# Forming the lower half of a weight slab with an accumulating DMA instead of a VectorE subtraction

## The chip, the cores and the metric

The kernel runs on one core of one Trainium2 chip. The metric is the device time of one execution in microseconds (us); lower is better. The engines are TensorE (PE: matmuls, and PEld: its weight loads), VectorE (DVE), ScalarE (ACT), GpSimd (POOL) and SyncE (SP). Weights come from HBM by DMA; most loads are issued on SP's queue, a few on POOL's.

## The reference

A token sequence of 512 positions with 1024 channels goes through two blocks. The first block, to which the change is confined, runs four mixers on the same normalised input and adds them up, each under its own gate. Cut to what matters:

```python
h = rms_norm(x, g) * (1 + scale) + shift        # scale and shift from c @ ada_w
p = h @ w_in                                    # 1024 -> all branches and their gates
y0 = rwkv7(p[A]) @ rwkv_out                     # branch A, a recurrent mixer
y1 = spatial_gating(p[B]) @ sg_out              # branch B: gelu, layer norm, 128x128 mixing
y2 = short_conv(p[C]) @ conv_out                # branch C: three taps
y3 = s5(p[D]) @ glu                             # branch D: a state space scan, then a GLU
acc = sum(sigmoid(p[gate b]) * y_b for b in range(4))
x = x + modulation * (acc @ w_o)                # then a feed forward, then the second block
```

All of it is float32, and the result is wanted close to float32 accuracy.

## The kernel before, in words

Every float32 product is made of three products of shorter numbers. An operand is split into an upper half `hi`, rounded to the type that PE multiplies at full speed, and a lower half `lo`, which is what the rounding left over. `mm3` (L169) adds hi·hi, hi·lo and lo·hi in PSUM; the lo·lo term is left out.

Weights come in slabs of 128 partitions by 1024 numbers (512 KB). `wload` (L140) loads one: SP starts the DMA into `raw` (four buffers), ACT copies it into `whi`, rounded (L152), and DVE writes `wlo` = `raw` - `whi` (L153). `whi` and `wlo` have three buffers each. The activations are split in the same way by `split` (`hi` and `lo`).

`_merge` (L813) handles the gate and the output of one branch: for each of eight tiles m it loads a `w_in` slab, makes 24 matmuls into `gp`, lets ACT take their tanh into `th` (L836), makes 6 matmuls with the branch's out slab into `yp` (12 for branch 3) and adds the product to `acc[m]` on DVE. An out slab (`conv_out`, `sg_out`, the GLU weights, `rwkv_out`) serves four tiles; a fresh one is loaded ahead of m = 0 and m = 4 and keeps one of the three buffers for that long. Ahead of each tile one or two `_ada` steps are made: a slab of `ada_w`, which uses the same four `raw` buffers, and a dot product with it on DVE (L328).

`_first_block` (L1165) runs `_start` (two slabs and the split of x), the seven projections of branch A, the tables of branch D begun, branch C, branch B, merge 2, the shift of branch A (fourteen dots), the tables of branch D, branch D itself, then the recurrence of branch A with merges 1 and 3 as fill between its steps, merge 0, and `w_o`. In branch B, `svp` are its projections, `sgz` a chain on DVE that normalises them, and `sgm` the mixing matmuls that read it (L928). In branch D, `s5k` are matmuls whose result is sent through HBM by POOL's queue (`s5_scr`, then eight and four small transfers `s5_ti`) and copied by DVE into a table `s5_toe`; `s5y` (L1138) are the matmuls that read the table.

A scheduler (Tile) fixes the order of the instructions of each engine from the program; each engine then works through its own list in order, and a transfer is started by the engine in whose list it stands. The order in which the calls are written, the dependences and the number of buffers decide what may run ahead.

Of the kernel before, what the change touches and what calls it, by code (L numbers as in the profile page):

```python
# [25 lines left out]
KD = 8  # L26
# [66 lines left out]
class _Core:  # L93


    WMAX = 1040

    def __init__(self, ctx, tc, dram):
        self.tc, self.nc, self.dram = tc, tc.nc, dram
        pool = lambda **kw: ctx.enter_context(tc.tile_pool(**kw))  # L100
        self.const = pool(name="const", bufs=1)
        self.small = pool(name="small", bufs=3)
        self.wpool = pool(name="w", bufs=1)
        self.tag, self.npool = {}, 0
        self.scratch = pool(name="scr", bufs=1, space=DRAM)
        self.tap = lambda name, ap: None
# [35 lines left out]
    def wload(self, src, kt, cols, tag=None):  # L142

        nc, n = self.nc, kt * cols
        raw = self.wpool.tile([128, self.WMAX], F32, name="raw", tag="raw", bufs=4)
        if tag is None:
            hi = self.wpool.tile([128, self.WMAX], F32R, name="whi", tag="whi", bufs=3)
            lo = self.wpool.tile([128, self.WMAX], F32R, name="wlo", tag="wlo", bufs=3)
        else:
            hi, lo = self.g("whi", tag, F32R), self.g("wlo", tag, F32R)  # L150
        nc.sync.dma_start(raw[:, :n], src)
        nc.scalar.activation(hi[:, :n], raw[:, :n], AF.Copy)  # L152
        nc.vector.tensor_tensor(lo[:, :n], raw[:, :n], hi[:, :n].bitcast(F32), OP.subtract)  # L153
        v = lambda t: t[:, :n].rearrange("p (k c) -> p k c", k=kt)
        return v(hi), v(lo)

# [11 lines left out]

    def mm3(self, out, w, x, first=True, last=True):  # L169

        n, total = 0, 3 * len(w)
        for (wh, wl), (xh, xl) in zip(w, x):
            for a, b in ((wh, xh), (wh, xl), (wl, xh)):
                self.nc.tensor.matmul(out, lhsT=a, rhs=b, start=first and n == 0, stop=last and n == total - 1)  # L174
                n += 1

    def proj(self, src, x, kt=8, name="mm", w=None):

# [635 lines left out]
def _merge(K, b, outs, acc, ada, halves=None):  # L814

    nc, d = K.nc, K.dram
    name = ("rwkv_out", "sg_out", "conv_out", "s5_glu_w")[b]
    first = b == 2  # L820
    w = {}
    for m in range(8):
        if m % 4 == 0:
            w[0] = K.wload(d[name][m // 4], 2, 512)
            if b == 3:
                w[1] = K.wload(d[name][2 + m // 4], 2, 512)
        cs = slice((m % 4) * 128, (m % 4 + 1) * 128)
        for _ in range(1 if first else 2):
            next(ada, None)
        wh, wl = K.wload(d["w_in"][19 + 8 * b + m], 8, 128)  # L830
        gp = K.mm("gp")
        for k in range(KD):
            K.mm3(gp, [(wh[:, k], wl[:, k])], K.h[k:k + 1], first=k == 0, last=k == KD - 1)
            yield
        th = K.g("th", "tm")
        nc.scalar.activation(th, gp, AF.Tanh, scale=0.5)  # L836
        yp = K.mm("yp")
        K.mm3(yp, [(w[0][0][:, k, cs], w[0][1][:, k, cs]) for k in range(2)], outs)
        if b == 3:
            y2 = K.mm("yp2")  # L840
            K.mm3(y2, [(w[1][0][:, k, cs], w[1][1][:, k, cs]) for k in range(2)], outs)
            sg = K.g("sg", "tm")
            nc.scalar.activation(sg, y2, AF.Tanh, scale=0.5)
            nc.vector.scalar_tensor_tensor(sg, sg, 1.0, yp, OP.add, OP.mult)
            nc.vector.scalar_tensor_tensor(th, th, 1.0, sg, OP.add, OP.mult)
            nc.vector.scalar_tensor_tensor(acc[m], th, 0.5, acc[m], OP.mult, OP.add)
        elif first:
            nc.vector.scalar_tensor_tensor(acc[m], th, 1.0, yp, OP.add, OP.mult)
        else:
            nc.vector.scalar_tensor_tensor(th, th, 1.0, yp, OP.add, OP.mult)  # L850
            nc.vector.tensor_tensor(acc[m], acc[m], th, OP.add)
        if halves is not None:
            halves.append(K.split(acc[m], "mg", 0.5))
        yield
# [310 lines left out]
def _first_block(K):  # L1165
    nc, d = K.nc, K.dram
    with ExitStack() as mix:
# [5 lines left out]
        with K.tags(e=9, e4=8):  # L1173
            with K.tc.tile_pool(name="s5", bufs=1) as sp:
                x, g1, rs = _start(K)
                tiles = _rwkv(K, x, g1, rs)
                last = K.last
                with K.tc.issue_after(K.split_1):
                    z = _s5_setup(K, sp)
                yc = _conv_branch(K)  # L1180
                yb = _sg_branch(K, last)
                acc = [K.g(f"acc{m}", "xr") for m in range(8)]
                for _ in _merge(K, 2, yc, acc, ada):
                    pass
                la, pairs = _rwkv_shift(K, tiles, rs)
                with K.tc.issue_after(last):
                    tab = _s5_tables(K, sp, z)
# [13 lines left out]
        tags(mg=16)  # L1201
        for _ in _merge(K, 0, ya, acc, ada, mg):
            pass
        for m in range(8):
            K.tap(f"acc{m}", acc[m])
        K.xr = _load(K, "x", 8, "xr")
# [464 lines left out]
```

## Time and profile before

| | us |
|---|---|
| median of 3 runs | 2149.45 (2147.0 to 2153.06) |
| the profiled execution | 2149.2 |
| its span in the profile | 2147.4 |
| PE busy | 2094.6 |
| DVE busy | 1416.1 |
| ACT busy | 934.1 |
| POOL busy | 23.5 |

The span is the time from the first to the last instruction of the profiled execution; what lies around it is 1.8 us. Busy times are sums over the span of each engine. The names on either side of an arrow in a row are tiles: `gp<-hi,wlo` is a matmul that reads `hi` and `wlo` and writes `gp`. "2.05 <-DVE wlo L153" in brackets is idle time of the engine ahead of the instruction, and what ended it. PEclk is the share of TensorE's full clock that was granted.

### The profile page before, as it was taken

Reading aid. Unit: us, or ns where it says so; the run is one execution under the profiler, and the core shown is the slowest. Engines: PE = TensorE matmul, PEld = TensorE weight load, DVE = VectorE, ACT = ScalarE, POOL = GpSimd, SP = SyncE. Lnnn points to the kernel's source line nnn. Section 1 sums busy time; section 2 is a strip of 40 time slices with the busy share of each in tenths; the row PEclk is TensorE's granted clock in tenths of the full one; section 3 lists DMA queues with packets and bytes.
Section 4 is the critical chain, followed back from the end, with each engine's and each line's share of the span. In section 5 each row is a group of like instructions: output and inputs, shape, how many; then the busy total and the mean of one; then the engine's idle time right before and its main releaser. Section 6 shows DMA issues by size and latency. Waiting matters only on the chain.

```text
span 2147.4 us, 29518 instructions
## 1 busy us (share of the span) xinstructions
PE 2094.6 (98%) x11502; PEld 1692.7 (79%) x11502; DVE 1416.1 (66%) x2655; ACT 934.1 (43%) x1549; POOL 23.5 (1%) x44
## 2 busy tenths in 40 slices
PE   6999999999999999999999999999999999999998
PEld 4877787888888888897778888888887778788887
DVE  7997884755734344558876756747568867575775
ACT  3334432333523232446764423324469944243433
POOL 0010000000000000000000000000000000000000
PEclk9999999999999999999999999999999999999999
DMA  8355441123322232232212222232321122323222
GB/s 329 106 182 180 159 148 50 60 84 133 108 98 89 98 98 89 99 119 89 80 50 98 98 93 94 89 98 81 128 79 40 60 79 86 101 83 105 97 81 67
DMA packets 68091, 220.47 MB, mean 103 GB/s; under 512 B 8068, under 2 KB 11060, under 8 KB 67952
## 3 DMA queue, kind: packets, MB, share of 16 engines
q1 hardware_dynamic: 64704, 210.19, 29.6%
q0 software_dynamic: 2096, 6.30, 1.0%
q8 instruction: 91, 1.49, 0.3%
q10 hardware_dynamic: 1152, 2.10, 0.3%
q14 instruction: 48, 0.39, 0.1%
HBM read 215.25 MB, written 3.30 MB: 102 GB/s over the span
## 4 chain that ended last, share of the span: by engine, by line
PE 85%; DVE 6%; ACT 4%; DMA 2%; issue 1%; DVEq 0%; ACTq 0%; SPq 0%
PE mm L174 62%; PE gp L174 7%; PE vt L174 3%; PE yp L174 2%; DMA raw<-ada_w 2%; PE pT L1336 1%; DVE wlo L153 1%; PE po L1349 1%; PE fin L174 1%; PE s L1316 1%; PE s L1317 1%; ACT whi L152 1%; DVE raw L328 1%; ACT p L1324 1%; PE pmt L643 1%
## 5 line engine op out<-in xcount | busy, mean ns | idle before, releaser
L174 PE MATMUL mm<-hi,whi 128*128 128x512 f32 x2088 | 829.7, 398 | 19.1 <-ACT hi L161 17.8
L174 PE MATMUL mm<-hi,wlo 128*128 128x512 f32 x2088 | 830.5, 398 | 1.1 <-DVE wlo L153 1.1
L174 PE MATMUL mm<-lo,whi 128*128 128x512 f32 x2088 | 829.2, 397 | 1.1 <-DVE lo L165 0.5
L152 ACT ACTIVATE whi<-raw 128x1024 fp32r<-128x1024 f32 (+3 forms) x341 | 350.3, 1030 | 754.9 <-PE mm L174 600.9
L153 DVE TENSOR_TENSOR wlo<-raw,whi 128x1024 fp32r<-128x1024 f32 (+3 forms) x341 | 403.5, 1186 | 180.2 <-ACT whi L152 170.7
L174 PEld LDWEIGHTS mm<-hi,whi 128*128 128x128 f32 x2088 | 395.7, 190 | 110.3 <-ACT hi L161 20.8
L174 PEld LDWEIGHTS mm<-lo,whi 128*128 128x128 f32 x2088 | 394.9, 189 | 91.1 <-DVE lo L165 2.7
L174 PEld LDWEIGHTS mm<-hi,wlo 128*128 128x128 f32 x2088 | 394.7, 189 | 89.9 <-DVE wlo L153 2.0
L1521 DVE TENSOR_TENSOR u<-mm,spr 128x512 f32<-128x512 f32 x88 | 60.6, 688 | 82.5 <-PE mm L174 82.2
L174 PE MATMUL gp<-hi,wlo 128*128 128x512 f32 x256 | 102.7, 401 | 3.3 <-DVE wlo L153 3.3
L174 PE MATMUL gp<-hi,whi 128*128 128x512 f32 x256 | 104.1, 407 | 0.9 <-ACT whi L152 0.9
L174 PE MATMUL gp<-lo,whi 128*128 128x512 f32 x256 | 102.9, 402 | 0.0
L1541 DVE TENSOR_TENSOR x<-x,mm 128x512 f32<-128x512 f32 x48 | 33.0, 687 | 96.1 <-PE mm L174 96.1
L1240 DVE SCALAR_TENSOR_TENSOR x<-mm,modv,x 128x512 f32<-128x512 f32 x32 | 24.0, 751 | 91.0 <-PE mm L174 91.0
L1522 ACT ACTIVATE cv<-u,vecs 128x512 f32<-128x512 f32 x88 | 71.3, 810 | 3.4 <-DVE u L1521 3.2
L1524 DVE SCALAR_TENSOR_TENSOR cv<-u,vecs,cv 128x510 f32<-128x510 f32 x88 | 66.0, 750 | 3.1
L1523 DVE SCALAR_TENSOR_TENSOR cv<-u,vecs,cv 128x511 f32<-128x511 f32 x88 | 65.6, 746 | 2.3 <-ACT cv L1522 2.1
L1532 ACT ACTIVATE cth<-cv 128x512 f32<-128x512 f32 x44 | 27.8, 632 | 86.2 <-DVE cv L1524 86.2
L174 PEld LDWEIGHTS gp<-hi,wlo 128*128 128x128 f32 x256 | 48.4, 189 | 15.6 <-DVE wlo L153 5.1
L1324 ACT ACTIVATE p<-p,at_m 128x128 f32<-128x128 f32 (+1 forms) x96 | 53.4, 557 | 14.7 <-DVE at_m L1323 13.7
L174 PEld LDWEIGHTS gp<-hi,whi 128*128 128x128 f32 x256 | 48.6, 190 | 13.4 <-ACT whi L152 1.8
L174 PEld LDWEIGHTS gp<-lo,whi 128*128 128x128 f32 x256 | 48.6, 190 | 10.6 <-issue 0.4
(532 smaller groups left out, 2612.1 us busy)
## 6 DMA issues: line engine op xcount, KB each, us to landing
raw<-w_up SPq DMA_DIRECT2D x88, 512.0 KB, 3.3
raw<-ffn_w SPq DMA_DIRECT2D x64, 512.0 KB, 3.3
raw<-w_in SPq DMA_DIRECT2D x49, 512.0 KB, 3.4
raw<-ada_w SPq DMA_DIRECT2D x32, 512.0 KB, 3.9
raw<-w_down SPq DMA_DIRECT2D x32, 384.0 KB, 3.1
ada_w<-ada_w SPq DMA_DIRECT2D x16, 512.0 KB, 8.7
raw<-w_out SPq DMA_DIRECT2D x16, 512.0 KB, 3.4
raw<-w_down SPq DMA_DIRECT2D x16, 512.0 KB, 3.3
```

Of the source, the lines that this page charges most:

```text
L152: nc.scalar.activation(hi[:, :n], raw[:, :n], AF.Copy)
L153: nc.vector.tensor_tensor(lo[:, :n], raw[:, :n], hi[:, :n].bitcast(F32), OP.subtract)
L174: self.nc.tensor.matmul(out, lhsT=a, rhs=b, start=first and n == 0, stop=last and n == total - 1)
L328: K.nc.vector.tensor_tensor_reduce(raw, raw, row, scale, 0.0, OP.mult, OP.add, out)
L1240: V.scalar_tensor_tensor(K.xr[m], ps, K.modv[:, 40 + m:41 + m], K.xr[m], OP.mult, OP.add)
L1324: A.activation(p[:, 0:n], p[:, 0:n], AF.Exp, bias=nm, scale=-1.0, accum_out=l)
L1521: V.tensor_tensor(u, ps, rs, OP.mult)
L1522: A.activation(c, u, AF.Identity, bias=K.vec("conv_b_2", l * 44 + j), scale=tap(2))
L1523: V.scalar_tensor_tensor(c[:, 1:], u[:, 0:S - 1], tap(1), c[:, 1:], OP.mult, OP.add)
L1524: V.scalar_tensor_tensor(c[:, 2:], u[:, 0:S - 2], tap(0), c[:, 2:], OP.mult, OP.add)
L1532: A.activation(th, gt, AF.Tanh, scale=0.5)
L1541: V.tensor_tensor(K.xr[m], K.xr[m], ps, OP.add)
```

## The change

A class attribute `lo_by_dma` is switched on behind `_start` and off behind merge 0. While it is on, `wload` lets ACT write the negated, rounded slab into the `wlo` tile, and a DMA on POOL's queue then adds the slab to it, read from HBM a second time. That makes the same difference, raw minus its rounded value. In the order of the change 59 slabs are formed in this way, 30.9 MB of further reads. `mm3` becomes a generator, `mm3_steps`, which yields after every third matmul; while the switch is on it places all terms that read `whi` first and all that read `wlo` last, over the whole sum rather than inside each step of k. `_merge` takes its 24 gate matmuls from one call of it.

```diff
--- before.py
+++ after.py
@@ -95,6 +95,8 @@
 
     WMAX = 1040
 
+    lo_by_dma = False
+
     def __init__(self, ctx, tc, dram):
         self.tc, self.nc, self.dram = tc, tc.nc, dram
         pool = lambda **kw: ctx.enter_context(tc.tile_pool(**kw))
@@ -150,7 +152,11 @@
             hi, lo = self.g("whi", tag, F32R), self.g("wlo", tag, F32R)
         nc.sync.dma_start(raw[:, :n], src)
         nc.scalar.activation(hi[:, :n], raw[:, :n], AF.Copy)
-        nc.vector.tensor_tensor(lo[:, :n], raw[:, :n], hi[:, :n].bitcast(F32), OP.subtract)
+        if self.lo_by_dma:
+            nc.scalar.activation(lo[:, :n], raw[:, :n], AF.Copy, scale=-1.0)
+            nc.gpsimd.dma_start(lo[:, :n], src, accum_op=OP.add)
+        else:
+            nc.vector.tensor_tensor(lo[:, :n], raw[:, :n], hi[:, :n].bitcast(F32), OP.subtract)
         v = lambda t: t[:, :n].rearrange("p (k c) -> p k c", k=kt)
         return v(hi), v(lo)
 
@@ -168,11 +174,19 @@
 
     def mm3(self, out, w, x, first=True, last=True):
 
-        n, total = 0, 3 * len(w)
-        for (wh, wl), (xh, xl) in zip(w, x):
-            for a, b in ((wh, xh), (wh, xl), (wl, xh)):
-                self.nc.tensor.matmul(out, lhsT=a, rhs=b, start=first and n == 0, stop=last and n == total - 1)
-                n += 1
+        for _ in self.mm3_steps(out, w, x, first, last):
+            pass
+
+    def mm3_steps(self, out, w, x, first=True, last=True):
+
+        terms = [((wh, xh), (wh, xl), (wl, xh)) for (wh, wl), (xh, xl) in zip(w, x)]
+        if self.lo_by_dma:
+            terms = [[t for a in terms for t in a[:2]], [a[2] for a in terms]]
+        terms = [t for a in terms for t in a]
+        for n, (a, b) in enumerate(terms):
+            self.nc.tensor.matmul(out, lhsT=a, rhs=b, start=first and n == 0, stop=last and n == len(terms) - 1)
+            if n % 3 == 2:
+                yield
 
     def proj(self, src, x, kt=8, name="mm", w=None):
 
@@ -829,9 +843,7 @@
             next(ada, None)
         wh, wl = K.wload(d["w_in"][19 + 8 * b + m], 8, 128)
         gp = K.mm("gp")
-        for k in range(KD):
-            K.mm3(gp, [(wh[:, k], wl[:, k])], K.h[k:k + 1], first=k == 0, last=k == KD - 1)
-            yield
+        yield from K.mm3_steps(gp, [(wh[:, k], wl[:, k]) for k in range(KD)], K.h)
         th = K.g("th", "tm")
         nc.scalar.activation(th, gp, AF.Tanh, scale=0.5)
         yp = K.mm("yp")
@@ -1173,6 +1185,7 @@
         with K.tags(e=9, e4=8):
             with K.tc.tile_pool(name="s5", bufs=1) as sp:
                 x, g1, rs = _start(K)
+                K.lo_by_dma = True
                 tiles = _rwkv(K, x, g1, rs)
                 last = K.last
                 with K.tc.issue_after(K.split_1):
@@ -1201,6 +1214,7 @@
         tags(mg=16)
         for _ in _merge(K, 0, ya, acc, ada, mg):
             pass
+        K.lo_by_dma = False
         for m in range(8):
             K.tap(f"acc{m}", acc[m])
         K.xr = _load(K, "x", 8, "xr")
```

The first place is on PE, in merge 2 (the short convolution's), around its fifth tile, where a fresh out slab is loaded. Before, in the order of PE (`gp_1404` is the fifth gate, `whi_1399` and `wlo_1400` its slab, `whi_1390` and `wlo_1391` the new out slab, `yp_1381` the fourth tile's output):

```order
L174 MATMUL yp_1381<-hi_865,whi_1207 128x512
L174 MATMUL yp_1381<-lo_866,whi_1207 128x512
L174 MATMUL yp_1381<-hi_865,wlo_1208 128x512
L174 MATMUL gp_1404<-hi_459,whi_1399 128x512
L174 MATMUL gp_1404<-lo_460,whi_1399 128x512
L174 MATMUL yp_1431<-hi_825,whi_1390 128x512
L174 MATMUL yp_1431<-lo_826,whi_1390 128x512
L174 MATMUL yp_1431<-hi_825,wlo_1391 128x512
L174 MATMUL gp_1404<-hi_459,wlo_1400 128x512
L174 MATMUL gp_1404<-hi_464,whi_1399 128x512
L174 MATMUL gp_1404<-lo_465,whi_1399 128x512
```

Of the change, the end of the fourth gate (`gp_1374`, whose slab has `wlo_1369`), the fourth output (`yp_1401`, with the old out slab) and the first of the fifth gate (`gp_1426`):

```order
L187 MATMUL gp_1374<-hi_483,wlo_1369 128x512
L187 MATMUL gp_1374<-hi_488,wlo_1369 128x512
L187 MATMUL gp_1374<-hi_493,wlo_1369 128x512
L187 MATMUL gp_1374<-hi_498,wlo_1369 128x512
L187 MATMUL yp_1401<-hi_835,whi_1222 128x512
L187 MATMUL yp_1401<-lo_836,whi_1222 128x512
L187 MATMUL yp_1401<-hi_876,whi_1222 128x512
L187 MATMUL yp_1401<-lo_877,whi_1222 128x512
L187 MATMUL yp_1401<-hi_835,wlo_1223 128x512
L187 MATMUL yp_1401<-hi_876,wlo_1223 128x512
L187 MATMUL gp_1426<-hi_463,whi_1420 128x512
L187 MATMUL gp_1426<-lo_464,whi_1420 128x512
```

and, after sixteen matmuls with `whi_1420`, the end of them and the first that reads the fifth gate's lower half, `wlo_1421`:

```order
L187 MATMUL gp_1426<-lo_494,whi_1420 128x512
L187 MATMUL gp_1426<-hi_498,whi_1420 128x512
L187 MATMUL gp_1426<-lo_499,whi_1420 128x512
L187 MATMUL yp_1453<-hi_835,whi_1410 128x512
L187 MATMUL gp_1426<-hi_463,wlo_1421 128x512
L187 MATMUL gp_1426<-hi_468,wlo_1421 128x512
L187 MATMUL gp_1426<-hi_473,wlo_1421 128x512
```

The third matmul of the fifth gate read `wlo` before; now the seventeenth does. From the last read of `wlo_1369`, whose buffer `wlo_1421` takes, to its first read there stand 23 matmuls.

The second place is on ACT, at the same slabs. Before (`th` is the tanh of a gate):

```order
L836 ACTIVATE th_1290<-gp_1265 128x512
L152 ACTIVATE whi_1390<-raw_1389 128x1024
L836 ACTIVATE th_1334<-gp_1309 128x512
L152 ACTIVATE whi_1399<-raw_1398 128x1024
L836 ACTIVATE th_1379<-gp_1354 128x512
```

Now:

```order
L154 ACTIVATE whi_1410<-raw_1409 128x1024
L848 ACTIVATE th_1353<-gp_1328 128x512
L156 ACTIVATE wlo_1411<-raw_1409 128x1024
L154 ACTIVATE whi_1420<-raw_1419 128x1024
L848 ACTIVATE th_1399<-gp_1374 128x512
L156 ACTIVATE wlo_1421<-raw_1419 128x1024
L154 ACTIVATE whi_1465<-raw_1464 128x1024
```

For each slab a negation, `wlo`, has come to stand behind the copy `whi`, for these slabs with the `th` of the tile before it in between.

The third place is on POOL, at the tables of branch D. Before (`s5_scr` and `s5_ti` are the transfers through HBM, MEMSET clears their target):

```order
L1045 MEMSET s5_ti0_1745 128x1024
L1041 DMA s5_scr_1743<-s5_kt_1741 128x256
L1048 DMA s5_ti0_1745<-s5_scr_1743 16x4x256
L1048 DMA s5_ti0_1745<-s5_scr_1743 16x3x256
L1048 DMA s5_ti0_1745<-s5_scr_1743 16x2x256
L1048 DMA s5_ti0_1745<-s5_scr_1743 16x256
L1045 MEMSET s5_ti1_1746 128x1024
L1048 DMA s5_ti1_1746<-s5_scr_1743 16x4x256 x5
```

Now:

```order
L157 DMA wlo_1858<-w_in 128x1024
L157 DMA wlo_1892<-w_in 128x1024
L1057 MEMSET s5_ti0_1770 128x1024
L157 DMA wlo_2198<-sg_out 128x1024
L1053 DMA s5_scr_1768<-s5_kt_1766 128x256
L1060 DMA s5_ti0_1770<-s5_scr_1768 16x4x256
L1060 DMA s5_ti0_1770<-s5_scr_1768 16x3x256
L1060 DMA s5_ti0_1770<-s5_scr_1768 16x2x256
L1060 DMA s5_ti0_1770<-s5_scr_1768 16x256
L157 DMA wlo_2211<-w_in 128x1024
L1057 MEMSET s5_ti1_1771 128x1024
L157 DMA wlo_2261<-w_in 128x1024
```

The accumulations stand among them: the two projections of branch D (`wlo_1858`, `wlo_1892`), the out slab of merge 1 (`wlo_2198`) and its first two gate slabs (`wlo_2211`, `wlo_2261`). On PE the matmuls `s5k`, on whose result `s5_scr` waits, stood ahead of merge 2 before, and stand behind it now.

## Rows read from the trace of the kernel before

**Rows 1.** The page's first part: busy time, share of the span, instructions of each engine.

```profile
PE 2094.6 (98%) x11502; PEld 1692.7 (79%) x11502; DVE 1416.1 (66%) x2655; ACT 934.1 (43%) x1549; POOL 23.5 (1%) x44
```

**Rows 2.** The page's chain that ended last, its share by engine.

```profile
PE 85%; DVE 6%; ACT 4%; DMA 2%; issue 1%; DVEq 0%; ACTq 0%; SPq 0%
```

**Rows 3.** PE's waits, 0 to 600 us: in total, times, longest.

```profile
PE sgm L928 <- DVE sgz L917: 3.4, 1, 3.4
PE gp L174 <- DVE wlo L153: 3.3, 3, 2.0
...
PE gp L174 <- ACT whi L152: 0.9, 1, 0.9
```

**Rows 4.** PE's timeline at sgm: start, duration, what, idle time before.

```profile
129.21 1.12 PE L928 MATMUL sgm<-sg_wsT,sgz 128*64 128x128 f32 x8 [3.43 <-DVE sgz L917]
...
131.28 0.63 PE L174 MATMUL mm<-hi,wlo 128*128 128x512 f32 x1
131.71 0.63 PE L174 MATMUL mm<-hi,whi 128*128 128x512 f32 x1
...
134.69 0.58 PE L174 MATMUL mm<-lo,whi 128*128 128x512 f32 x1
```

**Rows 5.** PE's timeline in merge 2.

```profile
168.77 0.40 PE L174 MATMUL yp<-hi,wlo 128*128 128x512 f32 x1
171.21 0.50 PE L174 MATMUL gp<-hi,wlo 128*128 128x512 f32 x1 [2.05 <-DVE wlo L153]
171.55 0.40 PE L174 MATMUL gp<-hi,whi 128*128 128x512 f32 x1
171.78 0.40 PE L174 MATMUL gp<-lo,whi 128*128 128x512 f32 x1
...
172.76 0.63 PE L174 MATMUL gp<-hi,wlo 128*128 128x512 f32 x1
...
175.32 0.63 PE L174 MATMUL gp<-hi,wlo 128*128 128x512 f32 x1
```

**Rows 6.** DVE's timeline at the same place.

```profile
168.18 1.23 DVE L328 CUSTOM_DVE_ANT_0 raw<-raw,c_row 128x1024 f32<-128x1024 f32 x1 [0.38 <-DMA raw<-ada_w]
...
169.94 1.22 DVE L153 TENSOR_TENSOR wlo<-raw,whi 128x1024 fp32r<-128x1024 f32 x1
```

**Rows 7.** Groups by line, 28 to 498 us: busy, mean ns, idle before.

```profile
L153 DVE TENSOR_TENSOR wlo<-raw,whi 128x1024 fp32r<-128x1024 f32 x61 | 74.4, 1221 | 39.6 <-ACT whi L152 36.0 <-PE yp L174 2.6 <-PE gp L174 0.5
L152 ACT ACTIVATE whi<-raw 128x1024 fp32r<-128x1024 f32 x62 | 65.6, 1059 | 137.4 <-PE gp L174 74.6 <-PE mm L174 33.2 <-issue 17.9
...
L836 ACT ACTIVATE th<-gp 128x512 f32<-128x512 f32 x32 | 18.7, 584 | 4.7 <-PE gp L174 4.6
```

**Rows 8.** One stretch: length, busy time of each engine, PEclk, DMA share, GB/s.

```profile
107.00:150.00 43.00, 39.53 (x232) 33.00 (x231) 41.36 (x126) 16.89 (x32) 7.90 (x14) 0.88 0.50 167
```

**Rows 9.** The page's DMA issues: count, size, median us to landing.

```profile
raw<-w_in SPq DMA_DIRECT2D x49, 512.0 KB, 3.4
...
raw<-w_down SPq DMA_DIRECT2D x32, 384.0 KB, 3.1
...
lora_r<-lora POOLq DMA_DIRECT2D x1, 384.0 KB, 3.7
```

**Rows 10.** Three stretches, DVE's subtractions of L153 alone, then PEclk, DMA share, GB/s.

```profile
54.00:107.00 53.00, 12.18 (x10) 1.00 0.32 105
119.00:198.00 79.00, 12.19 (x10) 0.91 0.55 180
198.00:288.00 90.00, 14.57 (x12) 1.00 0.51 168
```

**Rows 11.** PE's timeline at the start.

```profile
24.35 0.40 PE L174 MATMUL mm<-hi,wlo 128*128 128x512 f32 x1
26.52 0.74 PE L174 MATMUL mm<-hi,whi 128*128 128x512 f32 x2 [1.78 <-ACT hi L161]
```

**Rows 12.** POOL's timeline.

```profile
133.30 4.13 POOL L1048 DMA_DIRECT2D s_ti<-s_scr  x8 [0.29 <-POOL s_ti L1045]
```

## The prediction

> **What bounds the kernel now.** I read the page's engine line first: TensorE (PE) is busy 2094.6 of 2147.4 us, VectorE (DVE) two thirds, ScalarE (ACT) less than half, GpSimd (POOL) hardly [rows 1]. The chain that ended last says the same: PE holds 85% of it, DVE 6% [rows 2]. So work taken off DVE is worth nothing by itself. It pays only where PE stood still for DVE, and the change reaches only the first block. There PE's waits are the next view. Those that the weight path causes are short: 3.4 us for the spatial gate's DVE chain, 3.3 us in three waits for a `wlo`, and 0.9 us for a `whi` [rows 3].
>
> A wait costs more than its own length, because PE comes back at its lower clock. Behind the 3.4 us wait the pitch of a 128x512 matmul is 0.43 us (131.28 to 131.71), 1.2 GHz, for eleven matmuls until 134.69 [rows 4]. In steady running it is 0.23 us (171.55 to 171.78), 2.4 GHz. Behind the 2.05 us wait at 171.21 seven matmuls (172.76 to 175.32) run at the slow pitch [rows 5]. Each slow one costs 0.43 - 0.23 = 0.2 us: 11 x 0.2 = 2.2 us and 7 x 0.2 = 1.4 us. The cause at 171.21 is DVE's queue: the `wlo` subtraction at 169.94 stood behind the `_ada` dot of 168.18, which waited for its own slab [rows 6].
>
> **What is removed.** 59 subtractions of 1.22 us [rows 7], 72 us of DVE. Worth on PE's path: the `wlo` waits, 3.3 us + 1.4 us slow clock. The gate chain's wait, 3.4 + 2.2: DVE is busy 41.36 of 43 us in the stretch that holds it [rows 8], and without its subtractions the chain should be done in time. The `whi` wait, 0.9, because raw buffers no longer wait for DVE. Sum **11.2 us** at most.
>
> **What is added to ACT.** 59 negations, each about the 1.06 us of the `whi` copy [rows 7], 62 us. In the same stretch ACT is busy 16.89 of 43 us [rows 8], so the five or six negations that fall into it fit beside PE. If that cover were gone, the price would be 1.06 us at each slab.
>
> **What is added to the DMA.** Each lower half now comes through an accumulating DMA on POOL's queue. No row of before shows one, so I bound its landing time X. From below: a plain 512 KB load from SP lands in 3.4 us; a load from POOL's queue took 3.7 us for 384 KB where SP's took 3.1, so 0.6 more: X = 4.0 [rows 9]. From above, reading source and old content one after the other: 4.0 + 3.4 = 7.4. I take 5.6: the stretch from 119 to 198 moves 180 GB/s at a DMA share of 0.55 [rows 10], so all engines move 327 GB/s and pass 512 KB in 1.6 us; the add has to move the old content as well, one more such passage, while the fixed part of the latency is paid once. The Trainium skill, "Collectives: The Full Stack", section on the fold count and why AG, RS and AR differ, says that a reduction in the DMA reads two sources per result and so runs at half of a copy's rate; no run here shows that yet. By that rule the transfer's 1.6 us would become 3.2, again 5.6; if it does not hold, the lower bound does.
>
> Does anybody wait for X? Tile has three `wlo` buffers, so an accumulation can start when an older slab has been used, and must land before the first matmul that reads it. `mm3_steps` puts all `wlo` terms last, which gives 16 matmuls or 3.7 us more time. Between the end of the buffer's former use and the first read I count matmuls in the new order of PE, by the pitch above. In steady stretches that is two slabs, 10 to 16 us. Seven places are short. At the fifth tile of merges 2 and 0 a fresh out slab takes the third buffer, and only 23 matmuls lie between: 5.3 us. At the first tile of merge 3 I count 4.8 us; at four more places 7.0, 7.8, 7.9 and 8.1 us. From the free buffer to the issue pass a `th` (0.58) that stands ahead on ACT, the negation (1.06) [rows 7] and some 0.3 us of hops, my estimate from the gaps between a `whi` copy and its subtraction: 1.95 us; at merge 3 there is no `th`, 1.36 us. PE then waits 1.95 + X - lead:
> - X = 5.6: 2.25 + 2.25 at 5.3 us, 2.2 at 4.8 us, 0.5 at 7.0 us: 7.2 us. Two of these are as long as the wait of 171.21, so 2 x 1.4 of slow clock: 10.0 us.
> - X = 4.0: 0.65 + 0.65 + 0.56 = 1.9 us.
> - X = 7.4: 4.05 + 4.05 + 3.96 + 2.35 + 1.55 + 1.45 + 1.25 = 18.7 us, and five slow stretches of about 1.3: 25.3 us.
>
> **Moved steps.** The terms are reordered in the two first slabs too. PE has 24 matmuls ahead of the second half of x, and waits 1.78 us at 26.52 [rows 11]. In the new order it has 16 and stands still earlier, but the eight lacking ones are done afterwards at the same price: I count 0, from -1 to +2 us. POOL's queue is in order: two accumulations and the out slab of merge 1 now share it with the memsets and the small `s5_ti` transfers, and s5k moves behind merge 2 on PE. From s5k to the first s5y that needs the table PE has about 35 us of work in the new order (116 matmuls of 512 columns at 0.23 us, 26.7, and some 8 us of small ones, by my estimate); the table's way (eight issues in 4.13 us [rows 12], two landings and four DVE copies, estimate 15 to 20 us) fits in it. I count 0.
>
> **The sum.** 10.0 - 11.2 = -1.2 us on the profiled execution's 2149.2 us (span 2147.4 and 1.8 around it): **2148.0 us**. The median of the runs shown is 2149.45, 0.25 us away, so no correction. 0.3%, 6.4 us, is about what a measurement of this kernel tells from no change.
>
> **Rivals.**
> - *The accumulation is nearly as quick as a load* (X near 4.0). -11.2 + 1.9 = -9.3: **2140 us**, faster. For it: DMA share is only 0.32 to 0.55 in the stretches where the slabs are used [rows 10]. Against it: the add must read its destination.
> - *The accumulation is late at all seven short places* (X near 7.4). +25.3 - 11.2 = +14.1: **2163 us**, slower. It ends on the slow side from X of about 6.4 on, where the seven waits, with their slow stretches, pass 11.2 + 6.4 us. For it: `_ada` slabs, raw slabs and second readings meet in the same stretches; by two passages each, 10 accumulations (as many as subtractions now [rows 10]) from 119 to 198 add 32 us to 0.55 x 79 = 43.5, so 75.5 of 79 us are taken, and a full queue lengthens X. Against it: the many loads that wait for nobody can give way.
> - *The DMA engines are the bound.* If an accumulation costs three passages, 4.8 us, then 10, 10 and 12 of them, in the three stretches, need 17 + 48 of 53 us, 43.5 + 48 of 79, and 46 + 58 of 90 [rows 10]: over by 12, 12.5 and 14 us. **2187 us**, slower. For it: it needs only one passage more than I take. Against it: no row.
> - *POOL is late with its issues*, as a further cause of the second case. The row shows eight issues in 4.13 us, 0.52 each [rows 12], while DVE is busy 41.36 of 43 us [rows 8]; by it nothing is added. The Trainium skill, "SBUF — State Buffer", section on who interferes with whom, says that GpSimd cannot write descriptors while VectorE holds their shared ports in some of its operations. By that rule each issue at a short place could wait for one DVE operation, up to 1.2 us, so some 4 us on four places: 2152 us. The issues in the trace don't show it.
>
> **Chances.** Forecast within 0.3% of before: 0.38. Quick accumulation, 2140: 0.34. Late at the seven places, 2163: 0.20. DMA-bound, 2187: 0.08. So faster 0.34, same 0.38, slower 0.28. The range for 8 in 10 goes from 2137 (the lower bound, a start that gains 1 us, and spread of the runs) to 2170, which leaves out the DMA-bound case and a part of the first. The likeliest case alone: 2143 to 2154.
>
> **What would show it.** Right: the waits at sgm and behind the `_ada` dots are gone; PE waits for a DMA that writes `wlo` at the fifth tiles of merges 2 and 0 and at the first of merge 3, each about 2 us; accumulations land in about 5.6 us; DVE loses 72 us and ACT gains 62; DMA share between 119 and 198 rises to about 0.95. Wrong: a landing time outside 4.0 to 7.4 us, waits at every slab, a gate chain that is still late though DVE has less to do, or a table for s5y that arrives late because it stands behind an accumulation on POOL.

## The result, and the profile after

The change made the kernel slower: 2196.72 us median (2194.52 to 2197.36, 4 runs) against 2148.22 for the kernel before in the same session, ratio 1.0224 with an interval of 1.0208 to 1.0240. I had put 2148 first and a range up to 2170. The profiled execution has a span of 2192.7 us, 45.3 more than before.

The page after: busy time by engine, the DMA queues, the chain by engine, and DMA issues with their median time to landing.

```profile
PE 2105.1 (96%) x11502; PEld 1697.6 (77%) x11502; DVE 1354.7 (62%) x2596; ACT 993.1 (45%) x1608; POOL 74.4 (3%) x103
...
q0 software_dynamic: 10592, 37.24, 8.7%
...
PE 82%; DMA 6%; ACT 5%; DVE 4%; issue 3%; POOL 0%; SPq 0%; DVEq 0%; ACTq 0%; POOLq 0%
...
raw<-w_in SPq DMA_DIRECT2D x49, 512.0 KB, 5.1
wlo<-w_in POOLq DMA_DIRECT2D x47, 512.0 KB, 8.0
raw<-ada_w SPq DMA_DIRECT2D x32, 512.0 KB, 5.3
```

DVE is busy 61.4 us less and ACT 59.0 us more than before [rows 1]. The groups themselves come out as predicted: the subtractions fall by 72.1 us (403.5 for 341 on the page of before, 331.4 for 282 now), of which overlapping instructions hide a part in the engine's total, and the 59 negations take 62.2. PE executes the same 11502 matmuls in 10.5 us more, which is time at the lower clock (its mean over the span falls from 0.992 to 0.987 of full), and it stands still for 87.6 us (span less busy) where it stood still for 52.8: +34.8. An accumulation lands after 8.0 us in the median, where I took 5.6 and bounded it by 7.4. Loads that are not part of the change are later too: `raw<-w_in` 5.1 us instead of 3.4 [rows 9].

PE's waits after, 0 to 700 us, in total, times, longest:

```profile
PE gp L187 <- DMA wlo<-w_in: 22.6, 9, 6.0
...
PE s5c L1114 <- ACT s_ut L1108: 7.5, 1, 7.5
PE mm L187 <- ACT gl_s L263: 3.5, 1, 3.5
PE sgm L940 <- ACT sh_row L366: 2.7, 1, 2.7
PE mm L187 <- DMA wlo<-w_in: 2.4, 1, 2.4
...
PE gp L187 <- DVE acc L860: 1.4, 1, 1.4
```

The waits that I counted as removed [rows 3] look removed by name, and others stand in their place. 25.0 us in ten waits are for an accumulation, 7.5 us for ScalarE's `s_ut` at `s5c`, 3.5 us for a part of a gelu (`gl_s`), 2.7 us still at `sgm`.

Where the time goes is seen by when PE reaches the same work (first or last start, us):

| | before | after |
|---|---|---|
| first `sgm` | 129.2 | 129.3 |
| first gate matmul, merge 2 | 140.1 | 140.1 |
| last `s5d`, branch D | 240.5 | 261.1 |
| last `pu`, recurrence with merges 1 and 3 | 429.6 | 463.8 |
| last `gp<-hi,whi`, merge 0 | 495.8 | 540.1 |

Up to the first gate nothing is lost or won in sum; all of it is lost behind.

The clearest single wait is the fifth tile of merge 0. First PE's timeline of the kernel after, then ACT's and POOL's in the same window, start and duration ahead of each:

```profile
512.01 0.39 PE L187 MATMUL yp<-hi,whi 128*128 128x512 f32 x1
518.41 3.58 PE L187 MATMUL gp<-hi,wlo 128*128 128x512 f32 x8 [6.01 <-DMA wlo<-w_in]
...
526.72 2.03 PE L187 MATMUL gp<-hi,wlo 128*128 128x512 f32 x8
```

```profile
507.09 0.60 ACT L848 ACTIVATE th<-gp 128x512 f32<-128x512 f32 x1 [0.80 <-PE gp L187]
507.58 1.05 ACT L156 ACTIVATE wlo<-raw 128x1024 fp32r<-128x1024 f32 x1
```

```profile
508.93 0.88 POOL L157 DMA_DIRECT2D wlo<-w_in  x1 [5.29 <-ACT wlo L156]
```

The gate before it ends at about 507.0, `th` follows at 507.09, the negation at 507.58, and POOL issues at 508.93: 1.95 us from the free buffer to the issue, just as I had it. PE has its 5.3 us of other work and then waits until 518.41; the transfer took 9.4 us. 1.95 + 9.4 - 5.3 = 6.1, and the row says 6.01. The formula held, its X did not. The transfer had company: two loads of `w_o` and the next accumulation were issued between 508.66 and 510.8. The eight matmuls that follow take 3.58 us; where PE had not stood still eight take 2.0 us.

The other long wait, `s5c`, shows a second way. Timelines of the kernel after, by engine, for POOL, DVE, ACT and PE:

```profile
207.50 0.86 POOL L157 DMA_DIRECT2D wlo<-sg_out  x1 [1.03 <-ACT wlo L156]
209.24 0.58 POOL L1053 DMA_DIRECT2D s_scr<-s_kt  x1 [0.88 <-ACT s_kt L1051]
217.62 2.08 POOL L1060 DMA_DIRECT2D s_ti<-s_scr  x4 [7.80 <-DMA s_scr<-s_kt]
```

```profile
226.94 1.23 DVE L342 CUSTOM_DVE_ANT_0 raw<-raw,c_row 128x1024 f32<-128x1024 f32 x1 [5.13 <-issue]
...
228.09 0.76 DVE L1063 COPY s_toe<-s_ti 128x512 f32<-128x512 f32 x2
```

```profile
229.00 1.40 ACT L1108 COPY s_ut<-s5b 64x128 f32<-64x128 f32 x8 [7.80 <-DVE s_toe L1063]
```

```profile
230.46 1.11 PE L1114 MATMUL s5c<-k_ident,s_ut 64*128 64x64 f32 x8 [7.45 <-ACT s_ut L1108]
```

`s_scr` goes out behind the accumulation of 207.50 and lands only when POOL can go on at 217.62, 7.8 us later by the wait. The four `s_ti` transfers of the first half have landed by about 221.2. The table copies (L1063) stand on DVE behind the dot of 226.94, though. Its row names no releaser ("issue"), but its slab, issued at 220.3, landed 6.6 us later by the trace, at 226.9: here the dot came last, not POOL's queue. `s_ut` uses the buffer of `s_ti`, so ACT's copies at 229.00 wait for the table copies, and PE waits for them.

DVE's dots on `_ada` slabs, the row of before and the row of after, 28 to 545 us:

```profile
L328 DVE CUSTOM_DVE_ANT_0 raw<-raw,c_row 128x1024 f32<-128x1024 f32 x32 | 39.0, 1222 | 12.1 <-DMA raw<-ada_w 12.0
```

```profile
L342 DVE CUSTOM_DVE_ANT_0 raw<-raw,c_row 128x1024 f32<-128x1024 f32 x32 | 39.1, 1223 | 56.4 <-DMA raw<-ada_w 49.0 <-issue 6.2 <-ACT kt L605 1.0
```

The idle time ahead of the dots, spent on their slabs, has gone from 12.0 to 49.0 us, although DVE has 59 subtractions less to do.

### The profile page after: what moved, and what is told of

Read it like the earlier page. It is cut to its first block, busy times and chain, and to the rows that moved or that the text cites. A ratio compares the mean times of both kernels' runs of the same rounds, so it can differ in the third digit from the quotient of the medians.

```text
span 2192.7 us, 29611 instructions
## 1 busy us (share of the span) xinstructions
PE 2105.1 (96%) x11502; PEld 1697.6 (77%) x11502; DVE 1354.7 (62%) x2596; ACT 993.1 (45%) x1608; POOL 74.4 (3%) x103
## 4 chain that ended last, share of the span: by engine, by line
PE 82%; DMA 6%; ACT 5%; DVE 4%; issue 3%; POOL 0%; SPq 0%; DVEq 0%; ACTq 0%; POOLq 0%
PE mm L187 63%; PE gp L187 5%; DMA wlo<-w_in 3%; PE vt L187 3%; DMA raw<-ada_w 2%; PE yp L187 1%; PE pT L1350 1%; PE po L1363 1%; PE fin L187 1%; PE s L1330 1%; DMA w_t<-w_in_t 1%; PE s L1331 1%; ACT whi L154 1%; ACT p L1338 1%; PE pmt L657 1%
## 5 line engine op out<-in xcount | busy, mean ns | idle before, releaser
L187 PE MATMUL mm<-hi,wlo 128*128 128x512 f32 x2088 | 807.9, 396 | 2.4 <-DMA wlo<-w_in 2.4
L159 DVE TENSOR_TENSOR wlo<-raw,whi 128x1024 fp32r<-128x1024 f32 (+3 forms) x282 | 331.4, 1178 | 145.4 <-ACT whi L154 133.8
L187 PE MATMUL gp<-hi,wlo 128*128 128x512 f32 x256 | 73.3, 424 | 22.6 <-DMA wlo<-w_in 22.6
L342 DVE CUSTOM_DVE_ANT_0 raw<-raw,c_row 128x1024 f32<-128x1024 f32 x32 | 39.1, 1223 | 56.4 <-DMA raw<-ada_w 49.0
L156 ACT ACTIVATE wlo<-raw 128x1024 fp32r<-128x1024 f32 x59 | 62.2, 1054 | 5.5 <-PE mm L187 3.8
```

The lines of the kernel that those rows point to most:

```text
L156: nc.scalar.activation(lo[:, :n], raw[:, :n], AF.Copy, scale=-1.0)
L342: K.nc.vector.tensor_tensor_reduce(raw, raw, row, scale, 0.0, OP.mult, OP.add, out)
```

## The experiments

Theory A: an accumulation takes about 8 us in this kernel, so it is late wherever its buffer comes free late, and it fills the DMA engines. Theory B: the `_ada` slabs, late for that reason, stop DVE's queue. Rival C: the new order of matmuls and engines costs (C2: ACT's longer queue). Rival D: GpSimd's queue itself. Each kernel is the changed one with the edit shown; the edits are cut to the lines that matter (`...`). Tile orders the engines anew for each kernel, so an edit can also move other work; where I know of it, it is said.

**One part alone: the new order.**

```diff
-        if self.lo_by_dma:
+        if False:
             nc.scalar.activation(lo[:, :n], raw[:, :n], AF.Copy, scale=-1.0)
```

> One part alone: the new order of mm3 is kept (all whi terms first, then all wlo terms), the lower half comes from the VectorE subtraction as before. Theory A (the accumulations land in about 8 us, which is too late at the short places, and fill the DMA engines so that the _ada slabs land late): no accumulation, so none of the waits on a DMA that writes wlo; time 2138 to 2150 us. Rival C (the new order of the matmuls and of the engines, with s5k moved, costs the time): 2160 us or more, with waits on PE that before does not have.

2145.24 us, ratio 0.9978 (0.9966 to 0.9990): slightly faster than before. No wait for a `wlo` is left on PE in the first block. C falls for the order of the matmuls. Its other half is not tested here: s5k stands at 119.7 us in this kernel, ahead of merge 2 as before, and at 204.9 in the change.

**The negation without the DMA.**

```diff
-            nc.gpsimd.dma_start(lo[:, :n], src, accum_op=OP.add)
+            nc.vector.tensor_tensor(lo[:, :n], raw[:, :n], lo[:, :n].bitcast(F32), OP.add)
```

> ScalarE's negation is kept, and VectorE adds raw to it instead of the DMA. Order of the matmuls as in the change. Theory A: 2138 to 2155 us, ScalarE's 62 us more are hidden. Rival C2 (ScalarE, which now has copy, tanh and negation in one queue, is late): 2165 us or more, with PE waiting for whi or wlo at the slabs.

2151.68 us, ratio 1.0005 (0.9995 to 1.0016). ACT's 62 us cost 6 us against the run before it (in its trace PE waits 4.5 us for a `wlo`), far from the 48 us of the change. C2 falls as the cause.

**The other part alone: the DMA with the old order.**

```diff
-        if self.lo_by_dma:
+        if False:
             terms = [[t for a in terms for t in a[:2]], [a[2] for a in terms]]
```

> The accumulating DMA is kept, mm3 has its old order (the third matmul of a slab reads wlo, not the seventeenth). Theory A: 16 - 2 = 14 matmuls or 3.2 us less time at each slab, so the nine waits on wlo grow by about 3 us each and further slabs begin to wait: 2220 to 2245 us. Rival C (the new order is what costs): 2150 to 2185 us.

2289.69 us, ratio 1.0634 (1.0616 to 1.0652). The direction is A's, the size twice what I expected: not ten but 22 waits for an accumulation, 73.4 us, and PE's busy time at 2143.9 us, 49 us over before, from the slow clock behind these and other waits. The new order is what saves the change from this.

**A copy in place of the addition.**

```diff
-            nc.gpsimd.dma_start(lo[:, :n], src, accum_op=OP.add)
+            nc.gpsimd.dma_start(lo[:, :n], src)
```

> The DMA on GpSimd's queue copies the slab again instead of adding it; this leaves out the addition, so the lower half holds the whole slab. Queue, order, ScalarE's negation and the second reading of HBM are those of the change. Theory A, with two passages of an accumulation through the DMA engines (2.9 us of all 16, by the share of its queue, against 1.6 for a plain 512 KB load): landing falls from 8.0 to 5 to 6 us, DMA share from 119 to 198 us falls from 0.82 to about 0.7, waits on wlo fall from 25 us to under 8, time 2155 to 2175 us. Rival D (GpSimd's queue and the second reading are the cost, whatever the operation): landing 7 us or more and 2188 to 2200 us.

2165.08 us, ratio 1.0060 (1.0045 to 1.0075): some 32 of the 48 us are the addition as such. The order of every engine is the changed kernel's, row by row, so this is the cleanest of the comparisons. The 13 to 17 us that remain hold the second reading of the slabs, ACT's negations (6 us in the run that adds on DVE) and the moved table, whose wait at `s5c` is still there; I did not part them. From its page and its waits on PE:

```profile
q0 software_dynamic: 10592, 37.24, 5.1%
...
wlo<-w_in POOLq DMA_DIRECT2D x47, 512.0 KB, 5.0
```

```profile
PE gp L187 <- DMA wlo<-w_in: 8.1, 6, 4.0
PE s5c L1114 <- ACT s_ut L1108: 7.2, 1, 7.2
```

The queue's share falls from 8.7% to 5.1%. Of that 1.0% was there before (`q0 software_dynamic: 2096, 6.30, 1.0%` on the page of before), so 59 accumulations take (190.8 - 21.5) / 59 = 2.9 us of all 16 engines each, and 59 copies (110.3 - 21.5) / 59 = 1.5 us. PE's waits for `wlo` fall from 25.0 to 8.8 us.

**The cost by itself.** A kernel of probes: one transfer at a time, each behind the landing of the one before.

```diff
+        for r in range(5):
+            t = neg("acc_load")
+            raw = tile("raw_load", "raw")
+            nc.sync.dma_start(raw, dram["w_in"][7 + r])
+            nc.gpsimd.dma_start(t, dram["w_in"][1 + r], accum_op=OP.add)
+            use(t)
```

> The disputed cost by itself: none of the reference's work is done (zeros are written out). One 512 KB transfer at a time, each behind the landing of the one before: five accumulations, five plain copies on GpSimd's queue, five accumulations from SBUF, five accumulations of half the columns, five pairs of accumulations, five accumulations and five plain copies each with a load on SP's queue that starts at the same moment, as the next slab's load does in the change. Theory A1 (a lone accumulation is about as I predicted, 5 to 6.2 us, and the load that the same negation releases makes it 8): alone 5 to 6.2, with the load 7.3 to 8.2, plain 4 alone and 4.6 with the load. Rival A2 (the accumulation is slow by itself): 7 us or more alone. If the second reading of HBM counts, the accumulation from SBUF lands 1 us or more earlier than the one from HBM.

Its DMA issues, count, size, median us to landing (`acc` alone, `acc_raw` from SBUF, `acc_half` half the columns, `acc_load` and `plain_load` with a load that starts at the same moment, as in the diff):

```profile
acc<-w_in POOLq DMA_DIRECT2D x5, 512.0 KB, 5.3
...
plain_pool<-w_in POOLq DMA_DIRECT2D x5, 512.0 KB, 3.7
acc_raw<-raw POOLq DMA_DIRECT2D x5, 512.0 KB, 4.5
...
acc_load<-w_in POOLq DMA_DIRECT2D x5, 512.0 KB, 7.1
plain_load<-w_in POOLq DMA_DIRECT2D x5, 512.0 KB, 4.4
...
acc_half<-w_in POOLq DMA_DIRECT2D x5, 256.0 KB, 3.9
```

A1 holds, in one execution, with 7.1 beside a load just under its range. A lone accumulation takes 5.3 us, near my estimate of 5.6; a copy 3.7. With the load that the same negation sets free it takes 7.1 (6.6 to 8.1). Of the pairs, two were issued 0.9 and 1.0 us apart and took 7.9 with 9.4 us and 5.4 with 7.3; the others, 2.8 to 2.9 us apart, took 5.3 to 5.5 each. The half one gives an estimate of two parts: 256 KB less save 1.4 us, so on a straight line 512 KB cost 2.8 us and 2.5 us are fixed. From SBUF it is 0.8 us earlier than from HBM; the rule set 1 us as the sign of a costly second reading, so that is not decided.

**The small transfers of the table on SP's queue.**

```diff
-    nc.gpsimd.dma_start(scr, kt)
+    nc.sync.dma_start(scr, kt)
...
-            nc.gpsimd.dma_start(ti[x][o:o + 16, i0:4],
+            nc.sync.dma_start(ti[x][o:o + 16, i0:4],
```

> As the change, but the transfer of s5_kt to HBM and the twelve small s5_ti transfers are issued on SP's queue, so they stand behind no accumulation on GpSimd's. Rival D (GpSimd's queue makes the table late: s5_scr takes 7.8 us to land there instead of 2.7): the wait of s5c for ScalarE's s_ut, 7.5 us, goes, time 2184 to 2190 us. Theory B (the table copies stand on VectorE behind an _ada dot, whose slab lands late because the DMA engines are filled): the wait stays at 5 us or more, 2192 to 2200 us.

2193.00 us, ratio 1.0200 (1.0182 to 1.0218). The wait at `s5c` falls from 7.5 to 3.1 us, between the two; the `s5_scr` transfer still takes 7.0 us from SP. Of the whole 48 us the edit is worth at most 4: the intervals of this run and of the change overlap. How much of the wait is GpSimd's queue stays open, since DVE's order changed with the edit: the table copies stand behind 30 `_ada` dots here and behind 31 in the change, and now wait for `s_ti` itself.

**Dots that never wait.**

```diff
+        a, scale = (row, 0.1) if free else (raw, scale)
-        K.nc.vector.tensor_tensor_reduce(raw, raw, row, scale, 0.0, OP.mult, OP.add, out)
+        K.nc.vector.tensor_tensor_reduce(a, a, row, scale, 0.0, OP.mult, OP.add, out)
```

> As the change, but each _ada dot in the first block reads a tile that is always there, not the slab just loaded; the slabs are still loaded into their buffers, so the DMA work stays. This leaves out part of the modulation. VectorE then waits for no ada slab. Theory B (late _ada slabs stop VectorE's queue, and through it gelu, the gate chain and the s5 table): the waits at s5c (7.5), behind gl_s (3.5), sgm (2.7) and behind acc (1.4) go, with their slow clock: 2173 to 2184 us; the waits on wlo stay at 20 to 28 us. If only late accumulations count: 2190 us or more.

2190.64 us, ratio 1.0196 (1.0180 to 1.0213). A miss: the waits at `s5c`, `gl_s` and `sgm` go, but 5.9 us at `s5b` and 3.2 us behind `acc` come, and 23.6 us for accumulations stay. It also moves s5k back to its place ahead of the gate chain, so it doesn't isolate the dots. B alone is worth 6 us at most: the intervals of this run and of the change still touch.

**Off ahead of the merges.**

```diff
+                K.lo_by_dma = False
                 for _ in _merge(K, 2, yc, acc, ada):
```

> lo_by_dma is switched off ahead of merge 2: the projections of branches A, B and C have accumulations and the new order, the merges and branch D have neither. The trace of the change reaches its first gate at 140.1 us, as before does, so the whole loss lies behind it. Theory A: 2145 to 2153 us. If the early slabs leave a debt (late _ada slabs, moved dots): 2160 us or more.

2153.01 us, ratio 1.0014 (1.0001 to 1.0027): the fifteen early slabs cost next to nothing, the 44 from merge 2 on nearly all.

**Negation ahead of the copy.**

```diff
-        nc.scalar.activation(hi[:, :n], raw[:, :n], AF.Copy)
+        if not self.lo_by_dma:
+            nc.scalar.activation(hi[:, :n], raw[:, :n], AF.Copy)
         if self.lo_by_dma:
             nc.scalar.activation(lo[:, :n], raw[:, :n], AF.Copy, scale=-1.0)
             nc.gpsimd.dma_start(lo[:, :n], src, accum_op=OP.add)
+            nc.scalar.activation(hi[:, :n], raw[:, :n], AF.Copy)
```

> ScalarE makes the negation ahead of the copy, so each accumulation can start 1.06 us earlier, and the raw buffer, whose release starts the next slab's load, comes free 1.06 us later. Theory A: about 1 us off each of the nine waits on wlo, 25 down to about 16, time 2183 to 2191 us. If the accumulations are late by queueing alone (they finish when the DMA engines have room): no change, 2192 to 2199 us.

2190.99 us, ratio 1.0194 (1.0178 to 1.0210). The waits for accumulations fall to 13.7 us, as A has it, but little more than half of the 11 us comes out (5.7 us, and the intervals touch): waits for `acc`, `whi`, `cy` (at `svp`) and at `z` grew by 7 us together.

**A fourth `wlo` buffer.**

```diff
-        raw = self.wpool.tile([128, self.WMAX], F32, name="raw", tag="raw", bufs=4)
+        raw = self.wpool.tile([128, self.WMAX], F32, name="raw", tag="raw", bufs=3)
...
-            lo = self.wpool.tile([128, self.WMAX], F32R, name="wlo", tag="wlo", bufs=3)
+            lo = self.wpool.tile([128, self.WMAX], F32R, name="wlo", tag="wlo", bufs=4)
```

> The change with four buffers for wlo instead of three, paid with one of raw's four (three left). An accumulation can then start one slab earlier, 5.5 us and more. Theory A (they start too late for what they take): the waits on wlo fall from 25 us to under 8; the late _ada slabs and the table stay; time 2155 to 2178 us. Rival (the DMA engines are the bound, whenever a transfer starts): waits on wlo 18 us or more, 2188 us or more.

2177.18 us, ratio 1.0130 (1.0112 to 1.0148). The waits for accumulations fall from 25.0 to 9.3 us (I had said under 8), and the time by 20 us (11 us in the profiled execution, the longest of its four). From its waits on PE:

```profile
PE mm L187 <- DMA wlo<-w_in: 5.0, 2, 3.4
PE s5b L1105 <- ACT s5u L1097: 4.5, 1, 4.5
PE gp L187 <- DMA wlo<-w_in: 4.3, 1, 4.3
```

What remains is spread: 4.5 us at `s5b`, 3.5 at `hr_b`, 3.3 at `sgm`, 2.9 behind `acc`, all waits for DVE or ACT.

The edit did a second thing, which its reading has to allow for. From its page:

```profile
L156 ACT ACTIVATE wlo<-raw 128x1024 fp32r<-128x1024 f32 x59 | 61.8, 1054 | 28.2 <-DMA raw<-w_in 24.2
...
wlo<-w_in POOLq DMA_DIRECT2D x47, 512.0 KB, 7.3
```

With three `raw` buffers the negations wait for their slabs, and fewer accumulations have a load beside them: in the trace of the change 50 of 59 start within 0.6 us of a load of 256 KB or more, here 11. The landing time falls from 8.0 to 7.3 us, and four that have no large transfer beside them land after 5.3 to 5.4 us. So the earlier start and the freer engines are not parted by this run, while both speak for A.

**No `_ada` loads in the merges, with three buffers and with four.**

```diff
-    K.nc.sync.dma_start(raw, src)
+    if not free:
+        K.nc.sync.dma_start(raw, src)
```

> As the run with free dots, but the _ada slabs of the first block's merges are not loaded at all; this leaves out part of the modulation. The 59 accumulations stay. If the filled DMA engines are the rest of the loss: raw loads land in 4.5 us or less instead of 5.1 to 5.5, time 2160 to 2180 us against 2190.6 with the loads. If the order of the engines or the accumulation's own latency is the rest: 2184 us or more.

> No _ada loads in the merges, as in the run before (part of the modulation left out), and four wlo buffers beside three raw ones. If late accumulations and filled DMA engines are together the whole loss: waits on wlo under 6 us, time 2143 to 2160 us. If something else of the change costs (ScalarE's negations, GpSimd, the order): 2168 us or more, as in the run with four wlo buffers.

With three buffers 2196.13 us, ratio 1.0215 (1.0195 to 1.0236): no gain, a miss. With four 2153.56 us, ratio 1.0023 (1.0012 to 1.0033). PE's waits of the two kernels, three buffers first:

```profile
PE gp L187 <- DMA wlo<-w_in: 28.2, 8, 8.5
...
PE gp L187 <- DVE acc L862: 4.7, 1, 4.7
...
PE mm L187 <- DMA wlo<-w_in: 1.5, 1, 1.5
```

```profile
PE mm L187 <- DMA wlo<-w_in: 4.7, 2, 3.4
PE gp L187 <- DVE rk_sv L812: 3.5, 1, 3.5
PE gp L187 <- DMA wlo<-w_in: 3.0, 1, 3.0
```

The two causes lie one behind the other. With three buffers PE waits for accumulations also without the `_ada` loads (29.7 us, and they still land after 8.0 us; 53 of the 59 start beside some other load). Once a fourth buffer takes these waits away, the `_ada` loads and what waits for them are worth 2177.2 - 2153.6 = 23.6 us. With both gone the kernel stands 5.5 us over before, and ACT's negations, the accumulations, their DMA work and the order of the matmuls are all still in it. Two things weaken this pair. In both runs without loads s5k is back ahead of merge 2 (123.1 and 136.3 us), so the 23.6 us hold that move too. And the kernel before has its `_ada` loads, which no run takes off it: if it gained the 11.2 us of waits that I counted, 17 us of the change would be left (an estimate). I did not separate what the loads cost as traffic from what DVE's waits on them cost in that pair, nor find why the waits grew from 25.0 to 29.7 us without the loads.

**Versions for use.** The order alone, from the third slab on; and with it the DMA for branch B's four slabs only.

```diff
-        if self.lo_by_dma:
+        if self.wlo_last:
             terms = [[t for a in terms for t in a[:2]], [a[2] for a in terms]]
...
+        K.wlo_last = i > 0
         p = K.g("rp", "rk")
...
-                K.lo_by_dma = True
...
+                K.lo_by_dma = True
                 yb = _sg_branch(K, last)
+                K.lo_by_dma = False
```

> A version for use: the subtraction on VectorE as before, the whi terms first from the third slab on (the first two keep the old order, in which PE has 24 matmuls ahead of the second half of x), until merge 0. Expected from the reorder alone, 2145.2 us, and its start, 1 us longer than before's: 2140 to 2146 us, faster than before by 0.1 to 0.4%.

> As the version with the late reorder, and the four slabs of branch B alone are formed by the accumulating DMA, which takes 4.9 us of subtractions off VectorE just where the gate's chain is late (sgm waits 3.8 us with the reorder alone). Expected if that chain is short of VectorE: the wait falls under 1.5 us, 2136 to 2143 us. If the _ada dots are what holds it: no change against the version without, within 2 us.

The first (without the last two added lines) 2147.11 us, ratio 0.9983 (0.9974 to 0.9992); above what I expected: the late start brought nothing against the plain reorder. The second 2141.59 us, ratio 0.9957 (0.9944 to 0.9970), the fastest kernel here. From PE's waits, without the four slabs and with them:

```profile
PE sgm L942 <- DVE sgz L931: 5.3, 2, 5.0
PE s5y L1152 <- DVE s_xb L1143: 4.2, 2, 4.0
```

```profile
PE s5y L1152 <- DVE s_xb L1143: 2.9, 2, 2.7
PE sgm L942 <- DVE sgz L931: 2.2, 1, 2.2
```

With 4.9 us of subtractions off DVE at the right place the wait at `sgm` falls from 5.3 to 2.2 us, less than expected, the time as expected.

## Why the prediction was wrong

**What bounds the kernel, what is removed.** Right that only PE's waits count and that DVE's 72 us are worth nothing by themselves. Of the 11.2 us to gain, the `wlo` waits are there to be had, but by the order alone, which needs no DMA. The gate chain was not freed: 2.7 of its 3.4 us of waiting are still there. DVE's load was not all that held it. The dots, which got later, are the likely rest: with dots that wait for no slab the wait goes.

**The price of an accumulation.** The step that failed: X, the landing time of an accumulation, put at 5.6 us and at most 7.4. It was priced as if the transfer ran alone. Alone it takes 5.3 us, so the working was right for what it described. The Trainium skill, "Collectives: The Full Stack", section on the fold count, says of a ring collective's reduction that its two source reads halve a copy's rate; the runs agree for this transfer too, with 2.9 us of the engines for 512 KB beside 1.5 for the copy, 1.9 times. But the negation that lets the accumulation start is also the last reader of `raw`, and sets off the next slab's load at the same moment. The two share the engines, 7.1 us in the probe, 8.0 in the kernel. My upper bound of 7.4 came from another picture and was no bound. Eight accumulations of the changed kernel have just this one load and no other large transfer beside them; they land after 7.2 to 8.1 us, 7.8 in the median. So the gap to the probe is not more traffic, and stays open. By my own sum X = 8.0 gives 22.9 us of waits, 9.1 of slow clock (seven stretches of 1.3) and 11.2 off: 2170 us, an estimate. That is some 21 of the 48 us.

**The seven short places.** The sum 1.95 + X - lead was right, as the wait of 6.01 us shows, and so were the places at the fifth tiles and at the first of merge 3 (2.95, 6.01 and 5.20 us). PE's timelines of the kernel after at the first and the third of these:

```profile
169.63 0.47 PE L187 MATMUL gp<-hi,whi 128*128 128x512 f32 x1 [1.43 <-DVE acc L860]
...
176.73 3.66 PE L187 MATMUL gp<-hi,wlo 128*128 128x512 f32 x8 [2.95 <-DMA wlo<-w_in]
...
333.16 0.79 PE L187 MATMUL gp<-hi,wlo 128*128 128x512 f32 x1 [5.20 <-DMA wlo<-w_in]
```

At the first the sum gives 4.65 us with X = 8.0; the row has 2.95, most of the difference being the 1.43 us that PE had stood still for `acc` just before. The seven waits come to 22.9 us; measured are 25.0 in ten. That these totals are so near is in part luck: ten waits stand against seven places.

**The moved table, counted at 0.** I compared it with `s5y`, the reader of the table. The first to wait was `s_ut`, which takes the buffer of `s_ti`: 7.5 us. I had named the accumulations on POOL's queue as what could make it late. `s_scr` did take 7.8 us, but 7.0 from SP's queue too, and in this trace the dot ahead of the table copies on DVE came last.

**What was left out of the sum.** Every transfer was priced by itself, none by what it does to the others. The fuller engines made the `_ada` slabs late, DVE's queue waits for them in order, and gelu, the gate chain and the table copies wait behind. The run with four buffers and loads kept still lies 26 us over before, near the 27 us or so that X = 8.0 leaves unexplained.

**The rivals.** The slow ones had the sign: late accumulations (2163) and filled DMA engines (2187). The second is nearer in size, but by luck and not for its reason (and its 2187 left out the 11.2 us that the other cases take off): an accumulation takes two passages, not three, the DMA share from 119 to 198 us rose to 0.82 where I had 0.95, and the run with four buffers and no `_ada` loads, at a DMA share of 0.81 from 119 to 198 us, is back within 0.3% of before. That POOL is late with its issues: an issue takes 0.86 us instead of 0.52, in the kernel (0.85 to 0.98) and in the probe with DVE idle alike, so no wait for DVE is seen. The Trainium skill ("SBUF — State Buffer", who interferes with whom) has GpSimd blocked only by some of DVE's operations; no run here sets one of those against an issue.

**The chances.** 0.28 for slower, and a range that ended 27 us short: both followed from one X for the likeliest case, and from an upper X that left no room for two effects at once.

## What to carry to other kernels

Price a longer transfer together with the transfer that the same event sets off, and against the lead that its buffers leave: here 5.3 us alone, 8.0 in place, 5.3 of lead. Work taken off an engine that is not the bound pays only where that engine is late: four slabs moved gained, 59 lost. And before an operand is made in another way, try to read it later: with the lower halves read last, PE waits for no `wlo` in the first block, and no transfer was needed.

## What the runs showed of the hardware that I had not expected

An accumulating 512 KB DMA takes GpSimd 0.86 us to issue, a plain one 0.53. Its 5.3 us split, by an estimate from two sizes, into 2.5 that are fixed and 2.8 that go with the bytes, and it is 0.8 us earlier when its source is SBUF. A load that starts beside it adds 1.8 us in the probe. How much clock is lost behind waits: 49 us in the run with the old order, where PE stands still 91 us longer than before (143.4 against 52.8), 73 of them for accumulations.
